# Where the weight sums of a seven-product down projection are formed: at the transfer's landing, or after each split

## The chip, the core and the metric

The kernel runs on one core of a Trainium2 chip. Time is device microseconds of one execution. The engines named are those of the profile: PE (matmul) with its weight load PEld, DVE, ACT, POOL, and SP, which here only issues transfers. Each works through its own instructions in order.

## What is computed

One layer of a hybrid decoder block on 256 tokens of width 2048, all in float32: a gated feed-forward network (SwiGLU, 5632 wide), a layer norm, a mixer (recurrence and attention), a layer norm, a second SwiGLU network, a third norm, and a gated projection.

```python
def swiglu(x, w_gate, w_up, w_down):
    return (jax.nn.silu(x @ w_gate) * (x @ w_up)) @ w_down
...
        x = layer_norm(DEEPNORM_ALPHA * x + 0.5 * swiglu(x, ffn1_w_gate[i], ffn1_w_up[i], ffn1_w_down[i]),
...
        x = layer_norm(DEEPNORM_ALPHA * x + mix, ln2_g[i], ln2_b[i])
        x = layer_norm(DEEPNORM_ALPHA * x + 0.5 * swiglu(x, ffn2_w_gate[i], ffn2_w_up[i], ffn2_w_down[i]),
                       ln3_g[i], ln3_b[i])
        x = x + jax.nn.sigmoid(x @ w_ple_gate[i]) * (p[i] @ w_ple_proj[i])
```

The change touches the product with `w_down` of both networks alone.

## The kernel before

**Precision.** Every weight tile of 256 rows x 512 columns arrives in float32 as `raw` [128, 2, 512] (512 KB). ACT casts it to a rounded `hi` (L98), DVE subtracts (L104) to get the rest, `lo`. PE multiplies with parts: three matmuls where the weight is the moving operand (activation hi x `hi`, hi x `lo`, activation lo x `hi`), two where it is the stationary one.

**The plan.** `make_plan` lists all 804 weight tiles ("entries") in the order of their use. Three pointers run through it. `load` issues the transfers of an entry, 4 entries ahead of the cast (L80). `prepare_hi` and `prepare_lo` cast and split up to AHEAD = 7 entries ahead of PE, as far as SLOTS = 7 `hi` and `lo` tiles allow. `take` hands an entry to PE. `raw` tiles come from a pool of RAWS = 9, activations and their forms from a pool `work` of 12 wide tiles. The schedule is manual: each engine runs its instructions in the order in which this code emits them, and a tile of a pool is reused when its last readers are through.

**A feed-forward network.** The 5632 columns are worked in 11 chunks (c) of 512. A chunk has 8 gate entries and 8 up entries, each group of 8 filling four PSUM banks (`group_a`). There are eight banks. When a group ends, `evac_a` empties each bank: ACT copies half (L351), DVE adds the other half (L352). After each odd chunk the down projection of the pair of chunks is done in the seven-product form (2 x 2 blocks of tokens and of weights B11, B12, B21, B22), for two column halves n, which makes 14 products per pair; each has two entries (j), 12 moving matmuls each. `make_forms` makes the token forms with ACT (L63) and DVE (L64); `product` multiplies, and adds the bank to `acc` with DVE (L408, L410). The products are interleaved with the next two chunks: one after every two gate or up entries, and in the eleventh chunk one after every entry. The eleventh chunk's own product with `w_down` is done plainly at the end (`down_last`).

**The weight side of a product.** In the order of use: p1 takes B11, p5 B11 + B12, p3 B22, p6 the sum of p5 and p3, p7 B12 + B22, p2 B21, p4 the sum p5 + p3 + p2. For p5 and p7 the entry's load is a plain transfer by SP (L75), followed by a transfer by POOL that adds the second block to the tile as it arrives (L77, `accum_op`); that one starts when the first has landed. For p6 and p4 DVE adds p3's or p2's tile onto p5's tile right before the cast (L89).

**Boundaries.** After each network and after the mixer, `ln_norm` normalises (POOL makes `rs`, L474; DVE scales, L477) and the first three entries of the next part are split by POOL into tiles of `work`.

Of the kernel before, what the change touches and what calls it, by code (L numbers as in the profile page):

```python
# [5 lines left out]
F32 = mybir.dt.float32  # L6
# [3 lines left out]
ALU = mybir.AluOpType  # L10
AX = mybir.AxisListType

P = 128
# [17 lines left out]
MAGIC = 12582912.0  # L31
AHEAD = 7
SLOTS = 7
RAWS = 9
ORDER = ("p1", "p5", "p3", "p6", "p7", "p2", "p4")
LINE = 16
PI_IN = 3.1415925
# [2 lines left out]
class Block:  # L40
# [26 lines left out]
    def load(self, q):  # L67
        e = self.plan[q]
        if e.get("load"):
            e["load"]()  # L70
        if e.get("sum"):
            return
        e["raw"] = self.tile(self.wraw, [P, 2, 512], F32, "raw")
        for k in e["parts"]:
            self.nc.sync.dma_start(e["raw"][:, k, :], e["src"][:, k, :])  # L75
        if e.get("plus") is not None:
            self.nc.gpsimd.dma_start(e["raw"], e["plus"], accum_op=ALU.add)  # L77

    def prepare_hi(self, q):
        while self.loaded < min(len(self.plan), q + 4):  # L80
            self.load(self.loaded)
            self.loaded += 1
        e = self.plan[q]
        if e.get("split"):
            e["split"]()
        if e.get("sum"):
            a, b = e["sum"]
            e["raw"] = a["raw"]
            self.nc.vector.tensor_tensor(a["raw"], a["raw"], b["raw"], op=ALU.add)  # L89
        if e["work"]:  # L90
            e["hi"], e["lo"] = self.wide_r((P, 2, 512)), self.wide_r((P, 2, 512))
        else:
            o = LINE if e["stationary"] else 0
            e["hi"] = self.tile(self.whi, [P, 1024 + 4 * LINE], F32R, "hi")[:, o:o + 1024].rearrange("p (k c) -> p k c", k=2)
            e["lo"] = self.tile(self.wlo, [P, 2, 512], F32R, "lo")
            self.live += 1
        for k in e["parts"]:
            self.nc.scalar.copy(e["hi"][:, k, :], e["raw"][:, k, :])  # L98

    def prepare_lo(self, q):  # L100
        e = self.plan[q]
        eng = self.nc.gpsimd if e["pool"] else self.nc.vector
        for k in e["parts"]:
            eng.tensor_tensor(e["lo"][:, k, :], e["raw"][:, k, :], e["hi"][:, k, :].bitcast(F32), op=ALU.subtract)  # L104

    def advance(self, need=0):
        end = min(self.limit, self.taken + AHEAD)
# [46 lines left out]
    def make_plan(self):  # L154
# [3 lines left out]
        def add(w, r0, c0, n=1, **kw):  # L158
            for j in range(n):
                plan.append({"src": self.rows2(w, r0 + 256 * j, c0), "work": False, "pool": False,  # L160
                             "parts": [slice(0, 2)], "stationary": False, **kw})
# [21 lines left out]
        def blocks(w, r0, n):  # L183
            got = {}

            def entries(kind):
                for j in range(2):
                    r, c = r0 + 256 * j, n * 512
                    at = {"p1": (0, 0), "p2": (512, 0), "p5": (0, 0), "p3": (512, 512), "p7": (0, 512)}.get(kind, (0, 0))
                    add(w, r + at[0], c + at[1], kind=kind)  # L190
                    e = got[kind, j] = plan[-1]
                    if kind in ("p5", "p7"):
                        e["plus"] = self.rows2(w, r + (512 if kind == "p7" else 0), c + 512)
                    if kind in ("p6", "p4"):
                        e["sum"] = got["p5", j], got["p3" if kind == "p6" else "p2", j]

            return [lambda kind=kind: entries(kind) for kind in ORDER]

# [26 lines left out]
        q = len(plan)  # L225
# [188 lines left out]
    def make_forms(self, h0, h1):  # L414
        nc = self.nc
        a, b = slice(0, P), slice(P, 256)
        z = self.wide((P, 2, 4, P)), self.wide((P, 2, 4, P))
        s1, s2, s3, s4 = z[0][:, 0], z[0][:, 1], z[1][:, 0], z[1][:, 1]
        self.forms = {}

        def put(kind, src):
            f = self.forms[kind] = self.wide_r((P, 2, 4, P))
            self.split(f[:, 0], f[:, 1], src)

        self.products = [(kind, n) for n in (0, 2) for kind in ORDER]
        put("p1", h0[:, :, a])
        yield
        nc.vector.tensor_tensor(s1, h1[:, :, b], h0[:, :, b], op=ALU.subtract)
        put("p5", s1)
        yield  # L430
        nc.vector.scalar_tensor_tensor(s2, s1, -1.0, h0[:, :, a], op0=ALU.mult, op1=ALU.subtract)
        nc.vector.scalar_tensor_tensor(s4, s2, -1.0, h1[:, :, a], op0=ALU.mult, op1=ALU.subtract)
        put("p3", s4)
        yield
        put("p6", s2)
        yield
        nc.vector.tensor_tensor(s3, h0[:, :, a], h0[:, :, b], op=ALU.subtract)  # L437
        put("p7", s3)
        yield
        put("p2", h1[:, :, a])  # L440
        yield
        put("p4", h1[:, :, b])
# [406 lines left out]
    def build(self):  # L849
        tc = self.tc  # L850
        with (
            tc.tile_pool(name="wraw", bufs=RAWS) as self.wraw,
            tc.tile_pool(name="whi", bufs=SLOTS) as self.whi,
            tc.tile_pool(name="wlo", bufs=SLOTS) as self.wlo,
            tc.tile_pool(name="work", bufs=12) as self.work,
            tc.tile_pool(name="const", bufs=1) as self.const,
            tc.tile_pool(name="small", bufs=2) as self.small,
            tc.tile_pool(name="work1", bufs=6) as self.work1,
# [58 lines left out]
```

## Time and profile before

| | us |
|---|---|
| median of 3 runs | 2037.47 (2035.24 to 2038.23) |
| the profiled execution | 2040.81 |
| its span, first to last instruction | 2039.0 |
| PE busy | 1916.1 |
| DVE busy | 1523.5 |
| ACT busy | 1074.1 |
| POOL busy | 243.0 |

Times in the rows further down are counted from the start of the span. A line name such as L98 is a line of the kernel before. In a table of waits, "A <- B" reads: engine and line A stood idle until B was done; behind it total us, times, longest us. In a timeline the brackets hold the idle time before an instruction and what ended it. PEclk is the granted clock of PE as a share of 2.4 GHz, so 0.50 is its other level, 1.2 GHz. Some matmul records may be missing from the trace, so counts of matmuls in a window can differ by a few.

### The profile page before, as it was taken

How to read it: one execution, taken by the hardware profiler on the slowest of the kernel's cores; microseconds unless marked ns; L12 is line 12 of the kernel's file. 1: busy time of each engine (PE TensorE's matmuls, PEld its weight loads, DVE VectorE, ACT ScalarE, POOL GpSimd, SP SyncE). 2: the span in 40 equal slices, each digit the busy share in tenths (PEclk: the TensorE clock that was granted, in tenths of full speed). 3: DMA queues.
4: the chain of work that ended last, by engine and by line, in shares of the span. 5: the costliest groups of instructions: out<-in, count | busy, mean ns of one | idle time of the engine just before them, and what ended most of it. 6: DMA issues, size and time to landing. Idle time of an engine off the chain costs nothing.

```text
span 2039.0 us, 26876 instructions
## 1 busy us (share of the span) xinstructions
PE 1916.1 (94%) x10004; PEld 1630.9 (80%) x10004; DVE 1523.5 (75%) x1889; ACT 1074.1 (53%) x1440; POOL 243.0 (12%) x173
## 2 busy tenths in 40 slices
PE   8989999989898989999999999999998999978999
PEld 7878878878787777887888898787887887867787
DVE  6676877868776798667677867787778687777874
ACT  6554544545545465456655545554545454545562
POOL 0000000000000006101010430000000000000150
PEclk9999999999999999999999999999999999989999
DMA  9757676777678775765455666877686877678663
GB/s 358 228 168 246 221 245 194 247 219 252 197 233 249 202 251 175 227 186 155 142 179 187 206 197 168 255 219 225 218 266 185 244 230 243 194 220 235 223 200 108
DMA packets 227651, 438.21 MB, mean 215 GB/s; under 512 B 13873, under 2 KB 16577, under 8 KB 227521
## 3 DMA queue, kind: packets, MB, share of 16 engines
q1 hardware_dynamic: 204736, 391.40, 57.2%
q0 software_dynamic: 22784, 45.10, 12.3%
q8 instruction: 78, 1.28, 0.3%
q14 instruction: 53, 0.43, 0.1%
HBM read 434.35 MB, written 2.10 MB: 214 GB/s over the span
## 4 chain that ended last, share of the span: by engine, by line
PE 50%; DMA 19%; DVE 17%; issue 7%; ACT 5%; POOL 1%; SPq 0%; ACTq 0%; DVEq 0%; POOLq 0%
PE mm L245 50%; DMA raw<-in_ffn_w_down_dram 19%; DVE lo L104 9%; ACT hi L98 2%; DVE w L352 2%; DVE raw L89 2%; DVE acc L410 1%; ACT w L523 1%; DVE w L524 1%; ACT w L63 1%; DVE w L538 1%; DVE w L64 1%; DMA raw<-in_ffn_w_gate_dram 0%; POOL raw L77 0%; PE mm L487 0%
## 5 line engine op out<-in xcount | busy, mean ns | idle before, releaser
L98 ACT CAST hi<-raw 128x1024 fp32r<-128x1024 f32 (+1 forms) x786 | 794.3, 1047 | 729.8 <-DMA raw<-in_ffn_w_down_dram 259.1
L245 PE MATMUL mm<-xT,hi 128*128 128x512 f32 (+1 forms) x3216 | 1120.4, 394 | 47.9 <-DVE w L352 41.7
L104 DVE TENSOR_TENSOR lo<-raw,hi 128x1024 fp32r<-128x1024 f32 (+1 forms) x786 | 957.3, 1249 | 216.9 <-ACT hi L98 211.2
L245 PE MATMUL mm<-xT,lo 128*128 128x256 f32 (+1 forms) x3216 | 894.6, 278 | 0.3 <-DVE lo L104 0.3
L245 PEld LDWEIGHTS mm<-xT,hi 128*128 128x128 f32 x3216 | 610.8, 190 | 181.4 <-DVE w L352 47.0
L245 PEld LDWEIGHTS mm<-xT,lo 128*128 128x128 f32 x3216 | 612.4, 190 | 7.8 <-DVE lo L104 2.1
L245 PE MATMUL mm<-hi,w 128*128 128x512 f32 x1464 | 495.0, 402 | 57.1 <-ACT w L63 26.7
L245 PEld LDWEIGHTS mm<-hi,w 128*128 128x128 f32 x1464 | 280.8, 192 | 131.1 <-ACT w L63 29.1
L245 PE MATMUL mm<-lo,w 128*128 128x512 f32 x732 | 292.3, 399 | 0.0
L77 POOL DMA_DIRECT2D raw<-in_ffn_w_down_dram x80 | 95.7, 1200 | 1221.0 <-DMA raw<-in_ffn_w_down_dram 438.0
L245 PE MATMUL mm<-hi,xT 128*128 128x512 f32 (+1 forms) x544 | 168.7, 386 | 0.0
L245 PEld LDWEIGHTS mm<-lo,w 128*128 128x128 f32 x732 | 141.4, 193 | 24.6
L352 DVE TENSOR_TENSOR w<-mm,w 128x256 f32<-128x256 f32 x200 | 83.6, 419 | 89.5 <-ACT w L351 89.0
L245 PEld LDWEIGHTS mm<-hi,xT 128*128 128x128 f32 x544 | 101.3, 189 | 19.2
L245 PE MATMUL mm<-lo,xT 128*128 128x512 f32 (+1 forms) x272 | 104.0, 382 | 3.6 <-DVE lo L104 3.6
L410 DVE TENSOR_TENSOR acc<-acc,mm 128x512 f32<-128x512 f32 x124 | 84.4, 680 | 19.6 <-PE mm L245 19.5
L89 DVE TENSOR_TENSOR raw<-raw,raw 128x1024 f32<-128x1024 f32 x80 | 97.3, 1217 | 0.0
L64 DVE TENSOR_TENSOR w<-w,w 128x512 fp32r<-128x512 f32 (+1 forms) x78 | 51.7, 663 | 60.0 <-ACT w L63 59.8
L351 ACT COPY w<-mm 128x256 f32<-128x256 f32 x200 | 71.7, 365 | 20.9 <-PE mm L245 17.1
L63 ACT CAST w<-w 128x512 fp32r<-128x512 f32 (+1 forms) x78 | 46.4, 595 | 63.9 <-DVE w L437 25.9
L524 DVE TENSOR_TENSOR w<-w,w 128x256 f32<-128x256 f32 x88 | 38.0, 432 | 44.2 <-ACT w L523 44.2
L523 ACT ACTIVATE w<-w 128x256 f32<-128x256 f32 x88 | 36.8, 418 | 56.1 <-DVE w L352 56.1
(136 smaller groups left out, 836.9 us busy)
## 6 DMA issues: line engine op xcount, KB each, us to landing
raw<-in_ffn_w_down_dram SPq DMA_DIRECT2D x216, 512.0 KB, 5.9
raw<-in_ffn_w_up_dram SPq DMA_DIRECT2D x176, 512.0 KB, 5.5
raw<-in_ffn_w_gate_dram SPq DMA_DIRECT2D x175, 512.0 KB, 5.9
raw<-in_w_in_dram SPq DMA_DIRECT2D x88, 512.0 KB, 4.3
raw<-in_ffn_w_down_dram POOLq DMA_DIRECT2D x80, 512.0 KB, 9.5
raw<-in_w_out_dram SPq DMA_DIRECT2D x32, 512.0 KB, 4.6
raw<-in_w_ple_gate_dram SPq DMA_DIRECT2D x32, 512.0 KB, 5.9
w<-in_ln_g_dram SPq DMA_DIRECT2D x12, 256.0 KB, 6.7
```

The costliest lines, as they stand in the source:

```text
L63: self.nc.scalar.copy(hi, src)
L64: (self.nc.gpsimd if pool else self.nc.vector).tensor_tensor(lo, src, hi.bitcast(F32), op=ALU.subtract)
L77: self.nc.gpsimd.dma_start(e["raw"], e["plus"], accum_op=ALU.add)
L89: self.nc.vector.tensor_tensor(a["raw"], a["raw"], b["raw"], op=ALU.add)
L98: self.nc.scalar.copy(e["hi"][:, k, :], e["raw"][:, k, :])
L104: eng.tensor_tensor(e["lo"][:, k, :], e["raw"][:, k, :], e["hi"][:, k, :].bitcast(F32), op=ALU.subtract)
L245: self.nc.tensor.matmul(out, lhsT=lhsT, rhs=rhs, start=start, stop=stop, skip_group_check=True)
L351: self.nc.scalar.copy(c, bank[:, 256:])
L352: self.nc.vector.tensor_tensor(dst, bank[:, :256], c, op=ALU.add)
L410: self.nc.vector.tensor_tensor(a, a, bank, op=op)
L523: nc.scalar.activation(s, g, AF.Sigmoid)
L524: nc.vector.tensor_tensor(g, g, s, op=ALU.mult)
```

## The change

The sums of the weight blocks are formed in two long-lived tiles per pair of entries. p1's entry loads both B11 (`raw`) and B12 (`other`) by SP. Right behind p1's split DVE adds `other` onto `raw` (p5's sum), and POOL's transfer then adds B22 onto `other` (p7's sum). Behind p3's split DVE adds p3's tile onto `raw` (p6's sum). Behind p6's split POOL's transfer adds B21 onto `raw` (p4's sum). p5, p6, p7 and p4 load nothing of their own. DVE still makes 80 additions and POOL still issues 80 accumulating transfers; SP's loads of `w_down` go from 216 to 176. There is one more raw tile (10), loads run 5 entries ahead instead of 4, `work` has 11 tiles instead of 12, and the sums of tokens in `make_forms` lie in tiles of the small pool `qk` (3 tiles).

```diff
-RAWS = 9
+RAWS = 10
+LOOK = 5
...
     def load(self, q):
...
-        if e.get("sum"):
+        if e.get("of"):
             return
         e["raw"] = self.tile(self.wraw, [P, 2, 512], F32, "raw")
         for k in e["parts"]:
             self.nc.sync.dma_start(e["raw"][:, k, :], e["src"][:, k, :])
-        if e.get("plus") is not None:
-            self.nc.gpsimd.dma_start(e["raw"], e["plus"], accum_op=ALU.add)
+        if e.get("beside") is not None:
+            e["other"] = self.tile(self.wraw, [P, 2, 512], F32, "raw")
+            self.nc.sync.dma_start(e["other"], e["beside"])
+
+    def raw_sum(self, a, b):
+        self.nc.vector.tensor_tensor(a, a, b, op=ALU.add)
+
+    def raw_grow(self, a, src):
+        self.nc.gpsimd.dma_start(a, src, accum_op=ALU.add)
 
     def prepare_hi(self, q):
-        while self.loaded < min(len(self.plan), q + 4):
+        while self.loaded < min(len(self.plan), q + LOOK):
...
-        if e.get("sum"):
-            a, b = e["sum"]
-            e["raw"] = a["raw"]
-            self.nc.vector.tensor_tensor(a["raw"], a["raw"], b["raw"], op=ALU.add)
+        if e.get("of"):
+            e["raw"] = e["of"][0][e["of"][1]]
...
     def prepare_lo(self, q):
...
+        for f in e.get("after", ()):
+            f()
...
             def entries(kind):
                 for j in range(2):
-                    r, c = r0 + 256 * j, n * 512
-                    at = {"p1": (0, 0), "p2": (512, 0), "p5": (0, 0), "p3": (512, 512), "p7": (0, 512)}.get(kind, (0, 0))
-                    add(w, r + at[0], c + at[1], kind=kind)
-                    e = got[kind, j] = plan[-1]
-                    if kind in ("p5", "p7"):
-                        e["plus"] = self.rows2(w, r + (512 if kind == "p7" else 0), c + 512)
-                    if kind in ("p6", "p4"):
-                        e["sum"] = got["p5", j], got["p3" if kind == "p6" else "p2", j]
+                    entry(kind, j)
+
+            def entry(kind, j):
+                r, c = r0 + 256 * j, n * 512
+                b22, b21 = self.rows2(w, r + 512, c + 512), self.rows2(w, r + 512, c)
+                at = {"p2": (512, 0), "p3": (512, 512)}.get(kind, (0, 0))
+                add(w, r + at[0], c + at[1], kind=kind)
+                e = got[kind, j] = plan[-1]
+                p1 = got["p1", j]
+                if kind == "p1":
+                    e["beside"] = self.rows2(w, r, c + 512)
+                    e["after"] = [lambda: self.raw_sum(p1["raw"], p1["other"]), lambda: self.raw_grow(p1["other"], b22)]
+                elif kind == "p3":
+                    e["after"] = [lambda: self.raw_sum(p1["raw"], e["raw"])]
+                elif kind == "p6":
+                    e["after"] = [lambda: self.raw_grow(p1["raw"], b21)]
+                if kind in ("p5", "p6", "p4", "p7"):
+                    e["of"] = p1, "other" if kind == "p7" else "raw"
...
-        z = self.wide((P, 2, 4, P)), self.wide((P, 2, 4, P))
-        s1, s2, s3, s4 = z[0][:, 0], z[0][:, 1], z[1][:, 0], z[1][:, 1]
+        s1, s2, s4 = (self.tile(self.qk, [P, 4, P], F32, "qk") for _ in range(3))
...
+        s3 = self.tile(self.qk, [P, 4, P], F32, "qk")
         nc.vector.tensor_tensor(s3, h0[:, :, a], h0[:, :, b], op=ALU.subtract)
...
-            tc.tile_pool(name="work", bufs=12) as self.work,
+            tc.tile_pool(name="work", bufs=11) as self.work,
```

The instructions move on DVE and on SP. DVE before, in the first pair of FFN 1, from gate entries ahead of p6 to p6's second entry (`raw_162` and `raw_165` are p5's tiles, `raw_185` and `raw_189` p3's, `raw_194` and `raw_197` gate's):

```order
L104 TENSOR_TENSOR lo_204_1165<-raw_194_1113,hi_203_1164 128x1024
L89 TENSOR_TENSOR raw_162_947<-raw_162_947,raw_185_1062 128x1024
L104 TENSOR_TENSOR lo_209_1189<-raw_197_1119,hi_208_1188 128x1024
L89 TENSOR_TENSOR raw_165_970<-raw_165_970,raw_189_1088 128x1024
L104 TENSOR_TENSOR lo_212_1196<-raw_162_947,hi_211_1195 128x1024
```

Each addition stands one split ahead of the split of its own sum. DVE after, at the same product (`raw_140` and `raw_149` are p1's long-lived tiles, `raw_176` and `raw_187` p3's, `qk` and `w4` forms of the tokens):

```order
L110 TENSOR_TENSOR lo_200_1125<-raw_176_1035,hi_199_1124 128x1024
L82 TENSOR_TENSOR raw_140_791<-raw_140_791,raw_176_1035 128x1024
L65 TENSOR_TENSOR w4_203_1149<-qk_180_1042,w4_203_1149 128x512
L110 TENSOR_TENSOR lo_202_1145<-raw_187_1067,hi_201_1144 128x1024
L82 TENSOR_TENSOR raw_149_820<-raw_149_820,raw_187_1067 128x1024
...
L110 TENSOR_TENSOR lo_214_1201<-raw_140_791,hi_213_1200 128x1024
```

The two additions now stand behind p3's splits, four entries ahead of p6's own. DVE after, at p1 of the same block (`raw_141` and `raw_150` hold B12, `raw_153` is a gate entry's):

```order
L110 TENSOR_TENSOR lo_163_932<-raw_140_791,hi_162_931 128x1024
L82 TENSOR_TENSOR raw_140_791<-raw_140_791,raw_141_793 128x1024
L110 TENSOR_TENSOR lo_165_952<-raw_149_820,hi_164_951 128x1024
L82 TENSOR_TENSOR raw_149_820<-raw_149_820,raw_150_822 128x1024
L110 TENSOR_TENSOR lo_168_976<-raw_153_847,hi_167_975 128x1024
```

These two additions are new on DVE; they make p5's sums. SP before, at the second column half of the same pair (`raw_266`, `raw_269` are p1's tiles, `raw_279`, `raw_282` p5's, each of which gets a transfer by POOL as well):

```order
L75 DMA raw_266_1461<-in_ffn1_w_down_dram 128x2x512
L75 DMA raw_269_1484<-in_ffn1_w_down_dram 128x2x512
L75 DMA raw_273_1504<-in_ffn1_w_gate_dram 128x2x512
L75 DMA raw_276_1510<-in_ffn1_w_gate_dram 128x2x512
L75 DMA raw_279_1532<-in_ffn1_w_down_dram 128x2x512
L75 DMA raw_282_1555<-in_ffn1_w_down_dram 128x2x512
L75 DMA raw_285_1575<-in_ffn1_w_gate_dram 128x2x512
```

And SP after, at the same place (`raw_264`, `raw_268` are p1's tiles, `raw_265`, `raw_269` those beside them):

```order
L76 DMA raw_264_1440<-in_ffn1_w_down_dram 128x2x512
L79 DMA raw_265_1442<-in_ffn1_w_down_dram 128x2x512
L76 DMA raw_268_1464<-in_ffn1_w_down_dram 128x2x512
L79 DMA raw_269_1466<-in_ffn1_w_down_dram 128x2x512
L76 DMA raw_272_1488<-in_ffn1_w_gate_dram 128x2x512
L76 DMA raw_276_1508<-in_ffn1_w_gate_dram 128x2x512
L76 DMA raw_283_1556<-in_ffn1_w_gate_dram 128x2x512
L76 DMA raw_286_1577<-in_ffn1_w_gate_dram 128x2x512
L76 DMA raw_289_1583<-in_ffn1_w_down_dram 128x2x512
```

Four loads of `w_down` stand together at p1, and none for p5: the next one, `raw_289`, is p3's.

## Rows read from the trace of the kernel before

**Rows 1.** Page, part 1: busy us, share of the span, instructions.

```profile
PE 1916.1 (94%) x10004; PEld 1630.9 (80%) x10004; DVE 1523.5 (75%) x1889; ACT 1074.1 (53%) x1440; POOL 243.0 (12%) x173
```

**Rows 2.** Page, part 4: the chain that ended last, by engine.

```profile
PE 50%; DMA 19%; DVE 17%; issue 7%; ACT 5%; POOL 1%; SPq 0%; ACTq 0%; DVEq 0%; POOLq 0%
```

**Rows 3.** Waits of ACT, whole span: total us, times, longest us.

```profile
ACT hi L98 <- DMA raw<-in_ffn_w_down_dram: 259.1, 60, 10.5
...
ACT hi L98 <- DVE raw L89: 191.5, 78, 5.5
```

**Rows 4.** Waits of PE, whole span.

```profile
PE mm L245 <- DVE w L352: 42.0, 18, 3.5
PE mm L245 <- ACT w L63: 31.1, 13, 9.3
PE mm L245 <- DVE acc L410: 25.0, 14, 3.5
```

**Rows 5.** Timeline, 124 to 136, one stall: start, us, instruction, [idle before <- releaser].

```profile
124.77 1.19 POOL L77 DMA_DIRECT2D raw<-in_ffn_w_down_dram  x1 [5.29 <-DVE w L64]
...
133.93 1.04 ACT L98 CAST hi<-raw 128x1024 fp32r<-128x1024 f32 x1 [5.40 <-DMA raw<-in_ffn_w_down_dram]
...
135.28 0.42 DVE L352 TENSOR_TENSOR w<-mm,w 128x256 f32<-128x256 f32 x1 [4.91 <-ACT w L351]
...
135.75 0.50 PE L245 MATMUL mm<-xT,hi 128*128 128x512 f32 x1 [1.86 <-DVE w L352]
```

**Rows 6.** Transfers of L77 (POOL's count, issue ns; landing), then L75's landing.

```profile
L77 POOL DMA_DIRECT2D raw<-in_ffn_w_down_dram x80: 1180/1196/1412, 85.6 to 1866.0; - x80
...
DMA to landing us min/median/max: 5.9/9.5/13.4
...
DMA to landing us min/median/max: 3.0/5.6/13.0
```

**Rows 7.** Timeline of PE: starts of products.

```profile
112.53 0.40 PE L245 MATMUL mm<-hi,w 128*128 128x512 f32 x1
120.73 0.40 PE L245 MATMUL mm<-hi,w 128*128 128x512 f32 x1
...
380.71 0.50 PE L245 MATMUL mm<-hi,w 128*128 128x512 f32 x1 [0.87 <-ACT w L63]
...
672.31 0.39 PE L245 MATMUL mm<-hi,w 128*128 128x512 f32 x1
677.79 0.42 PE L245 MATMUL mm<-hi,w 128*128 128x512 f32 x1
```

**Rows 8.** Windows: us, busy us (instructions) by engine, PEclk, DMA share, GB/s.

```profile
104.33:653.90 549.57, 515.54 (x2706) 439.64 (x2704) 415.42 (x487) 280.06 (x356) 38.20 (x32) 0.98 0.74 226
1256.14:1801.24 545.10, 514.02 (x2706) 438.20 (x2704) 415.46 (x487) 278.16 (x355) 38.25 (x32) 0.98 0.74 227
653.90:756.66 102.76, 86.23 (x411) 71.08 (x409) 85.00 (x98) 55.12 (x69) 7.16 (x6) 0.92 0.78 228
1801.24:1906.29 105.05, 87.48 (x411) 71.61 (x409) 85.11 (x98) 55.23 (x69) 7.15 (x6) 0.90 0.76 221
178.80:240.40 61.60, 61.60 (x337) 53.31 (x336) 49.62 (x58) 30.93 (x40) 4.77 (x4) 1.00 0.78 246
175.40:178.80 3.40, 3.40 (x11) 2.90 (x11) 3.30 (x8) 3.31 (x5) 0.00 (x0) 0.50 0.00 0
```

**Rows 9.** Timeline of the last chunk of FFN 1: ACT and PE.

```profile
657.99 1.04 ACT L98 CAST hi<-raw 128x1024 fp32r<-128x1024 f32 x1 [2.97 <-DMA raw<-in_ffn_w_down_dram]
...
662.20 0.79 PE L245 MATMUL mm<-hi,w 128*128 128x512 f32 x1 [8.13 <-ACT w L63]
```

**Rows 10.** Page, part 5: DVE's additions, busy us and mean ns.

```profile
L89 DVE TENSOR_TENSOR raw<-raw,raw 128x1024 f32<-128x1024 f32 x80 | 97.3, 1217 | 0.0
```

**Rows 11.** Timeline of the third boundary: POOL and PE.

```profile
1921.70 2.39 POOL L104 TENSOR_TENSOR w<-raw,w 128x1024 fp32r<-128x1024 f32 x1 [2.42 <-issue]
...
1925.34 0.63 PE L487 MATMUL mm<-ident,acc 128*128 128x128 f32 x4 [0.83 <-DVE acc L477]
```

## The prediction

> **What bounds the kernel now.** I read the busy shares first: PE is busy 94% of the span, DVE 75%, ACT 53% [rows 1]. So PE is the engine to keep fed, and the question is who makes it stop. The chain of waits answers: after PE (50%) its largest part is DMA, 19% [rows 2], although plain weight loads are issued far ahead. The table of ACT's waits names the transfers: ACT's cast (`hi`) stood 259.1 us, 60 times, behind transfers of `w_down` [rows 3]; PE's own table names only near neighbours, L352, L63 and L410, together 98.1 us [rows 4]. One stall in the timeline joins them [rows 5]: POOL issues an accumulating transfer at 124.77; ACT, which works in order, stops 5.40 us at the cast that needs it and goes on at 133.93; the copy L351 that empties a PSUM bank stood behind that cast, so DVE's L352 waited 4.91 for it; PE waited 1.86 for the bank. Why always these transfers: an accumulating one starts only when the plain load of the same tile has landed, and then takes 5.9 / 9.5 / 13.4 us (min / median / max) itself, behind loads that take 3.0 / 5.6 / 13.0 [rows 6]; the cast wants it two products later at most.
>
> **What the stalls cost.** A product and two gate/up entries on clean ground take 120.73 − 112.53 = 8.20 us; in the last chunk a product and one entry take 677.79 − 672.31 = 5.48 [rows 7]. So an entry is 2.72 and a product 2.76. A pair of chunks, from its first product to the next pair's, is 32 entries and 14 products: 125.7. The fourth pair of an FFN ends an entry earlier (123.0). The last chunk, from its first product on, is 15 entries and 14 products: 79.4. Against that [rows 8]: the four pairs of FFN 1 took 549.57 where 3 × 125.7 + 123.0 = 500.1, 49.5 too long; those of FFN 2 545.10, 45.0 too long; the last chunks 102.76 and 105.05, 23.4 and 25.7 too long. In all 143.6 us. It holds the 98.1 of waits and some 45 of lost clock: after a stop the granted clock is 0.50 for a while, as in 175.40 to 178.80, where 11 matmuls took the whole 3.40 us [rows 8].
>
> **The change, part by part.**
>
> *p5 and p7.* Their second half no longer comes by a transfer that ACT meets on arrival. B11 and B12 are both plain loads, made with p1; DVE adds them for p5; POOL grows the second tile to p7's sum, four products (16 entries in the order of the plan) before it is cast. In time: 16 entries at a quarter of a slot, 8.20 / 4 = 2.05 us, are 33 us, against a landing of 13.4 at worst [rows 6]. This takes ACT off the transfers in pairs, at all three places where it stood. The chunk entries between are now ahead of what they need, and I take the pairs down to their clean length but for 2 us each: a short wait of 0.87 as at 380.71, which follows ACT's form casts and no transfer [rows 7], and part of a stretch at half clock behind it. Estimate: 8 × 2 = 16 stay, 94.5 − 16 = **78.5 gained**. Bounds: 94.5 if nothing stays; about half if the waits for banks are DVE's own (first rival).
>
> *p6 and p4.* p6's addition on DVE moves forward to p3's `lo`, so ACT's 191.5 us behind additions [rows 3] lose their cause; these waits are mostly slack that ACT has, since PE's table shows little behind them, so I count nothing. p4's sum becomes an accumulating transfer, issued behind p6's `lo`, 11 entries or 23 us ahead of its cast in the pairs. In the last chunk the lead is 9 entries of 5.48 / 3 = 1.83, 16.4 us, against 13.4 plus two issues of 1.2 [rows 6]: just enough.
>
> *The last chunk.* Its worst stop is PE's 8.13 at 662.20, behind a cast that waited for a transfer at 657.99 [rows 9]; such stops go too. But DVE is busy 85.00 of these 102.76 us, and 85.11 of 105.05 [rows 8], and its work stays: as many additions, 80 of 1217 ns [rows 10], splits and evacuations as before. So DVE is what is late next, and the floor is 85, not 79.4. I take 88 (97% busy; bounds 85 and 95, the second at DVE 89%): 14.8 + 17.0 = **31.8 gained**.
>
> *Does DVE hold the pace in the pairs?* From 178.80 to 240.40 no transfer is waited for: PE was busy 61.60 of 61.60 us with DVE at 49.62 (81%), through a change of group [rows 8]. So 81% on DVE need not stop PE.
>
> *Loads.* 40 plain loads of 512 KB fall away (p5 and p7 shared a start with p1's tile); the accumulating transfers stay 80. The DMA share in the clean stretch is 0.78, and nobody waited for plain loads there: worth nothing on the path. The tenth raw tile and the look-ahead of 5 instead of 4 entries pay for two pairs of tiles that now live through five to seven products. In the built order SP's plain loads stay at least 8 entries ahead of their cast (7 before), 16 us against 13.0 at worst [rows 6].
>
> *One work tile fewer.* At the three boundaries POOL splits three entries into work tiles. At the third boundary one already waited for its tile and ran 2.39 us at 1921.70, ahead of the small `rs` on POOL; PE lost 0.83 to it at 1925.34 [rows 11]. With 11 tiles the built order puts one such split late at boundaries 1 and 2 (0.83 each) and a second one at the third (2.4 more): 4.1. In the mixer one DVE operation gains a wait on POOL, for which no row stands: I take 1, between 0 and the 2.39 of that split, since it is a product of two tiles of the same size. Together **5.1 lost**, between 0 (the tiles come free in time) and 8 (a full split of 2.39 at each boundary and the mixer's 1).
>
> **Sum.** 78.5 + 31.8 − 5.1 = 105.2. The profiled execution took 2040.8 (span 2039.0 and 1.8 around it), which becomes 1935.6; it is 3.4 above the median of the runs, so I forecast 2037.5 − 105.2 = 1932.3.
>
> **A rule against it.** PE stops for banks that DVE and ACT empty late [rows 4]. The Trainium skill, "Perfetto Trace Analysis", section Optimization Strategy, says that consistent bubbles, the same gap repeating on the engine that should be saturated, can mean that SBUF or PSUM has no room for the next tile. By that rule the cure would be banks, not transfers. The mechanism here would be: eight banks, four of a group and up to three of products, so that the next group's first bank waits for L352 or L410 whatever ACT meets. The clean stretch speaks against it, since a group changes in it with no stop.
>
> **Rivals.**
> 1. *DVE's order.* The added sums stand directly behind a `lo` on DVE, 1.2 us each, two in a row per product, and L352 and L410 stand behind them; or p4's transfer, with its narrow lead, is late in the last chunk. For: DVE has 18% to spare in the pairs and next to none in the last chunk. Against: the clean stretch has p6's additions in it. If half of the waits for L352 and L410 stays, half of (42.0 + 25.0) / 98.1 of the 110.3 gained is lost, 38: **1970** (1955 to 2000).
> 2. *Banks* (the mechanism beside the rule). All of those waits stay, 68% of the gain: 75 lost, **2008**.
> 3. *Nothing moves.* As many accumulating transfers go through POOL as before; if they queue behind DVE and now hold ACT at p4 and p7 instead of p5 and p7, the stalls change place only: **2037**. Against: 23 and 33 us of lead.
> 4. *Slower: raw tiles.* Four of the ten tiles are held from p1 to p4 and two of them to p7, so loads of gate and up rotate through six. If a load is issued later than 13.0 / 2.05 = 6.3 entries before its cast, the stall of today meets every entry. Price: 20 blocks (two column halves of ten pairs), two extra stops each, of some 4 us (a wait of 1.86 [rows 5] and about as much again at half clock): 160, less the 110: **2087**. Against: the lead of 8 in the built order, which holds only if the tiles come free on time.
>
> **How the numbers follow.** My forecast has 0.64 (1910 to 1950: 85 in the last chunks and nothing left in the pairs on one side, 95 in the last chunks and 8 of boundary cost on the other), a better time than 1910 has 0.02, DVE's order 0.17, banks 0.06, nothing moves 0.04, raw tiles 0.07. The range runs from 1908 to 1990: it holds the forecast and most of the first rival and leaves out some 0.2. Faster by over 0.2% (about what a measurement of this kernel can tell from no change): 0.64 + 0.02 + 0.17 + 0.06 = 0.89; the same 0.04; slower 0.07.
>
> **What would show it.** In the profile after: ACT's waits for `w_down` transfers near 0 instead of 259.1, with still 80 accumulating transfers; a pair of 127 to 128 us and a last chunk near 88 with DVE over 95% busy; PE's waits for L352 and L410 (other line numbers then) down to a few us; the granted clock near 1.00 in the FFNs; at the boundaries a POOL split ahead of `rs` and a stop of PE of 1 to 3 us. If ACT's waits for transfers vanish and those for banks stay, the banks or DVE's order were the cause, and pairs stay over 130. If ACT waits for gate and up loads, the raw tiles are too few. If ACT still waits for `w_down`, the leads are wrong.

## The result and the profile after

The changed kernel takes 1921.0 us (median of 4 runs, 1920.29 to 1922.0), the kernel before, beside it, 2037.85: a ratio of 0.9425 (95% interval 0.9407 to 0.9442), 5.8% less time. The forecast was 1932. The profiled execution took 1922.0 us with a span of 1919.9, against 2039.0 before.

The page of the profile after, its parts 1 and 4 (the chain of waits by engine):

```profile
PE 1878.9 (98%) x10004; PEld 1614.0 (84%) x10004; DVE 1522.9 (79%) x1889; ACT 1090.7 (57%) x1440; POOL 242.4 (13%) x173
...
PE 87%; DVE 7%; issue 2%; ACT 2%; DMA 1%; POOL 1%; SPq 0%; ACTq 0%; DVEq 0%; POOLq 0%
```

DVE, ACT and POOL are about as busy in microseconds as before [rows 1]; what went is PE's time: it stands idle for 41.0 us of the span instead of 122.9, 81.9 less, and its busy time is 37.2 less for the same matmuls, since fewer of them run at half clock (PEclk below). DMA has left the chain: 1% instead of 19% [rows 2], PE itself has 87% of it. ACT's waits and then PE's, whole span (total us, times, longest us):

```profile
ACT hi L104 <- DVE raw L82: 16.4, 10, 2.1
...
ACT hi L104 <- DMA raw<-in_ffn_w_down_dram: 7.9, 6, 1.8
```

```profile
PE mm L263 <- DVE acc L428: 11.0, 4, 3.5
PE mm L263 <- DVE xT L65: 5.2, 1, 5.2
PE mm L505 <- DVE acc L495: 4.8, 3, 3.1
PE mm L263 <- ACT w L64: 4.3, 6, 0.7
```

ACT's 259.1 us behind growing tiles are 7.9, its 191.5 behind additions 16.4 [rows 3]. PE's waits for L352 (now L370) are gone from the table, those for L63 (now L64) are 4.3 instead of 31.1, those for L410 (now L428) 11.0 instead of 25.0 [rows 4]. POOL still issues 80 accumulating transfers; they land in 5.7 / 7.4 / 11.0 us instead of 5.9 / 9.5 / 13.4 [rows 6]:

```profile
L85 POOL DMA_DIRECT2D raw<-in_ffn_w_down_dram x80: 1180/1196/1665, 97.0 to 1755.4; - x80
...
DMA to landing us min/median/max: 5.7/7.4/11.0
```

Windows of the same four stretches as [rows 8], from first product to first product (us, busy us and instructions by engine, PEclk, DMA share, GB/s): the four pairs of each network, then the two last chunks.

```profile
104.89:606.54 501.65, 500.27 (x2706) 432.50 (x2705) 422.48 (x500) 292.01 (x364) 38.31 (x32) 1.00 0.80 235
1197.00:1697.00 500.00, 500.00 (x2706) 432.25 (x2705) 420.52 (x497) 290.87 (x363) 38.28 (x32) 1.00 0.80 234
606.54:695.39 88.85, 82.90 (x410) 69.58 (x409) 77.17 (x87) 51.27 (x61) 7.22 (x6) 0.96 0.82 243
1697.00:1784.78 87.78, 81.82 (x411) 68.80 (x409) 77.19 (x87) 51.28 (x61) 7.22 (x6) 0.98 0.83 247
```

In the four pairs of the second network PE is busy for 500.00 of 500.00 us, at full clock. The account of the spans, term by term:

| | before | after | gained | forecast |
|---|---|---|---|---|
| four pairs, FFN 1 | 549.57 | 501.65 | 47.9 | |
| four pairs, FFN 2 | 545.10 | 500.00 | 45.1 | |
| pairs together | | | 93.0 | 78.5 |
| last chunks | 102.76 + 105.05 | 88.85 + 87.78 | 31.2 | 31.8 |
| all the rest | 736.5 | 741.6 | -5.1 | -5.1 |
| span | 2039.0 | 1919.9 | 119.1 | 105.2 |

### The profile page after: what moved, and what is told of

It is laid out like the page before. It is cut to its first block, busy times and chain, and to the rows that moved or that the text cites. A ratio compares the mean times of both kernels' runs of the same rounds, so it can differ in the third digit from the quotient of the medians.

```text
span 1919.9 us, 26885 instructions
## 1 busy us (share of the span) xinstructions
PE 1878.9 (98%) x10004; PEld 1614.0 (84%) x10004; DVE 1522.9 (79%) x1889; ACT 1090.7 (57%) x1440; POOL 242.4 (13%) x173
## 4 chain that ended last, share of the span: by engine, by line
PE 87%; DVE 7%; issue 2%; ACT 2%; DMA 1%; POOL 1%; SPq 0%; ACTq 0%; DVEq 0%; POOLq 0%
PE mm L263 86%; DVE lo L110 3%; DVE raw L82 1%; DVE w L370 1%; ACT hi L104 1%; DMA raw<-in_w_in_dram 0%; DMA raw<-in_ffn_w_gate_dram 0%; PE mm L505 0%; DVE w L556 0%; ACT w L64 0%; POOL w L110 0%; DVE w L65 0%; DMA raw<-in_ffn_w_down_dram 0%; DVE acc L495 0%; DVE acc L428 0%
## 5 line engine op out<-in xcount | busy, mean ns | idle before, releaser
L104 ACT CAST hi<-raw 128x1024 fp32r<-128x1024 f32 (+1 forms) x786 | 809.6, 1049 | 545.3 <-PE mm L263 470.6
L263 PE MATMUL mm<-xT,hi 128*128 128x512 f32 (+1 forms) x3216 | 1104.8, 390 | 6.2 <-DVE xT L65 5.2
L263 PE MATMUL mm<-hi,w 128*128 128x512 f32 x1464 | 483.2, 394 | 13.3 <-DVE acc L428 11.0
L263 PEld LDWEIGHTS mm<-hi,w 128*128 128x128 f32 x1464 | 276.5, 189 | 76.2 <-ACT hi L104 13.7
L428 DVE TENSOR_TENSOR acc<-acc,mm 128x512 f32<-128x512 f32 x124 | 84.9, 684 | 100.8 <-PE mm L263 100.8
L370 DVE TENSOR_TENSOR w<-mm,w 128x256 f32<-128x256 f32 x200 | 83.6, 419 | 28.1 <-ACT w L369 27.6
L82 DVE TENSOR_TENSOR raw<-raw,raw 128x1024 f32<-128x1024 f32 x80 | 97.8, 1222 | 1.4
L64 ACT CAST w<-qk 128x512 fp32r<-128x512 f32 (+1 forms) x42 | 25.5, 609 | 83.6 <-DVE qk L455 40.4
L542 DVE TENSOR_TENSOR w<-w,w 128x256 f32<-128x256 f32 x88 | 38.0, 432 | 43.4 <-ACT w L541 43.4
L508 ACT ACTIVATE qk<-mm,par 128x128 f32<-128x128 f32 x96 | 36.1, 456 | 54.3 <-PE mm L505 54.1
```

Of the source, the lines that this page charges most:

```text
L64: self.nc.scalar.copy(hi, src)
L82: self.nc.vector.tensor_tensor(a, a, b, op=ALU.add)
L263: self.nc.tensor.matmul(out, lhsT=lhsT, rhs=rhs, start=start, stop=stop, skip_group_check=True)
L370: self.nc.vector.tensor_tensor(dst, bank[:, :256], c, op=ALU.add)
L428: self.nc.vector.tensor_tensor(a, a, bank, op=op)
L508: nc.scalar.activation(z[:, q, :], bank[:, q * P:(q + 1) * P], AF.Identity, bias=self.par[:, p0 + 16 + kb:p0 + 17 + kb], scale=self.par[:, ...
```

## The experiments

Twelve kernels ran, four at a time on one chip. The kernel before took 2043.64 us beside the first four, 2037.79 beside the second and 2038.34 beside the third, so ratios to it are compared across groups.

### Is it the growing tile? The second transfers left out

```diff
-        if e.get("plus") is not None:
-            self.nc.gpsimd.dma_start(e["raw"], e["plus"], accum_op=ALU.add)
```

> The kernel before, with the accumulating second transfers of p5 and p7 left out (B12's share in p5's sum and B22's in p7's are missing; all else stands, the additions of p6 and p4 right ahead of their casts too). Theory (ACT stood at casts whose tile was still growing): pairs fall from 137 to 126 us, the last chunks from 103 to about 88, and no boundary cost is added: 1915 us, or a little less than the changed kernel's 1921. Rival, the places of DVE's additions: what ACT waits behind them (191.5 us) stays and holds pairs above 130: 1950 to 1970. Rival, banks: PE's waits for L352 and L410 stay near 67 us: about 1990.

Measured: 1911.28 us, ratio 0.9357 (0.9342 to 0.9371). Its windows, one pair and one last chunk:

```profile
606.82:692.27 85.45, 80.76 (x410) 67.53 (x409) 79.51 (x89) 50.11 (x61) 0.00 (x0) 1.00 0.66 219
...
231.51:357.52 126.01, 125.97 (x682) 108.68 (x681) 105.67 (x126) 72.37 (x91) 0.00 (x0) 1.00 0.64 217
```

and its waits, ACT's behind the additions and PE's longest:

```profile
ACT hi L96 <- DVE raw L87: 173.5, 72, 4.0
```

```profile
PE mm L243 <- DVE acc L408: 8.3, 6, 2.6
```

The stalls are gone, with the additions of p6 and p4 where they were and with the same eight banks. So those additions and the banks were not what stopped PE. Both rivals fall. What this run cannot tell is whether the transfers' traffic or their landing counted, since it takes both away.

### Lead or traffic? p7's transfer issued later

```diff
                 if kind == "p1":
...
-                    e["after"] = [lambda: self.raw_sum(p1["raw"], p1["other"]), lambda: self.raw_grow(p1["other"], b22)]
+                    e["after"] = [lambda: self.raw_sum(p1["raw"], p1["other"])]
...
                 elif kind == "p6":
-                    e["after"] = [lambda: self.raw_grow(p1["raw"], b21)]
+                    e["after"] = [lambda: self.raw_grow(p1["other"], b22), lambda: self.raw_grow(p1["raw"], b21)]
```

> The changed kernel with one thing moved: POOL's transfer that grows p7's tile is issued behind p6's split, 4 entries (8.2 us) ahead of its cast instead of 16; the traffic is the same. Theory (the lead of the transfer against its landing of 5.9 to 13.4 us decides): ACT's waits for w_down transfers come back, at p7 alone, 20 blocks of some 2 to 3 us of PE each: 1960 us (1940 to 1985). Rival, 21 MB less traffic or the deeper loads made the gain: 1921, pairs stay at 125.7.

Measured: 2008.8 us, ratio 0.9832 (0.9815 to 0.9848). ACT's wait, and the windows of a pair and of a last chunk:

```profile
ACT hi L104 <- DMA raw<-in_ffn_w_down_dram: 169.9, 25, 12.1
```

```profile
238.88:370.59 131.71, 127.79 (x683) 110.08 (x681) 105.98 (x126) 72.60 (x91) 9.67 (x8) 0.99 0.77 224
630.37:735.03 104.66, 86.17 (x410) 71.74 (x409) 77.43 (x87) 50.63 (x61) 8.48 (x7) 0.92 0.73 209
```

The same instructions and bytes, one transfer of two issued 12 entries later, and some seven tenths of the gain are lost: lead, not traffic. The direction was as expected, the loss was twice as large and outside the range given. A last chunk loses all that it had gained (104.66 against 102.76 in the kernel before): the lead of 4 entries in the pairs is there one of 3 entries, 3 x 1.83 = 5.5 us, less than the quickest landing, 5.9 in the kernel before [rows 6] and 5.8 in this one.

The same transfer issued behind p3's split, in the middle:

```diff
                 if kind == "p1":
...
-                    e["after"] = [lambda: self.raw_sum(p1["raw"], p1["other"]), lambda: self.raw_grow(p1["other"], b22)]
+                    e["after"] = [lambda: self.raw_sum(p1["raw"], p1["other"])]
                 elif kind == "p3":
-                    e["after"] = [lambda: self.raw_sum(p1["raw"], e["raw"])]
+                    e["after"] = [lambda: self.raw_sum(p1["raw"], e["raw"]), lambda: self.raw_grow(p1["other"], b22)]
```

> The changed kernel with p7's growing transfer issued behind p3's split: 8 entries ahead of its cast (16 us in the pairs, 6 entries or 11 us in the last chunk) instead of 16; with 4 entries the time was 2009 us. Theory (lead against a landing of 7 us at the median and 11 to 14 at worst): pairs stay at 125.7, the last chunks rise to 90 to 95: 1925 us (1920 to 1937). Rival, order on POOL and SP rather than the lead: pairs already rise above 128, 1945 or more.

Measured: 1922.82 us, ratio 0.9431 (0.9416 to 0.9445); the changed kernel beside it on that chip 1922.78 (0.9433, 0.9414 to 0.9452). Last chunks:

```profile
607.28:696.01 88.73, 82.77 (x411) 69.50 (x409) 77.18 (x87) 51.28 (x61) 7.22 (x6) 0.96 0.81 243
1697.60:1785.48 87.88, 81.95 (x411) 68.83 (x409) 77.18 (x87) 51.29 (x61) 7.22 (x6) 0.98 0.82 248
```

8 entries of lead are as good as 16, and in the last chunk 6 (11 us) as good as 12, where I had expected a few us of waiting. So between 4 and 8 entries lies the point from which the lead is enough. The run of the changed kernel that it was measured against:

> The changed kernel once more, as the measure for the three runs beside it on the same chip: 1921 us; pairs 125.7, last chunks 88 to 89.

It took 1922.78 us (1919.76 to 1927.55). The profiled execution was the slowest of them, 1927.55. Its pairs in FFN 1 took 501.65 us as before, but its last chunks more than the 88 to 89 expected:

```profile
606.07:695.63 89.56, 83.61 (x411) 70.02 (x409) 77.45 (x87) 51.40 (x61) 7.22 (x6) 0.96 0.81 241
1697.04:1787.51 90.47, 84.53 (x410) 70.79 (x409) 77.53 (x87) 51.29 (x61) 7.22 (x6) 0.94 0.81 237
```

So last chunks of one and the same kernel lie between 87.78 and 90.47 us.

### The sizes alone, and the sums alone

All of the change's sizes on the kernel before: 10 raw tiles, loads 5 entries ahead, 11 work tiles, token sums in `qk` (the two diffs below, together):

> The kernel before with the change's sizes alone: 10 raw tiles, loads 5 entries ahead instead of 4, 11 work tiles, the token sums in the small pool; the transfers and sums as before. Theory: the accumulating transfers start one entry (2.05 us) earlier, which takes 2 of the 4 us or so of each of ACT's 60 waits, so a third of the loss goes, and the boundaries cost 5: about 2000 us (1980 to 2025). Rival, that depth of loading is what the change gained by: 1921 to 1935. Rival, sizes do nothing: 2038 to 2043.

Measured: 1968.36 us, ratio 0.9637 (0.9621 to 0.9652). That is a gain of some 74 us, and more than I gave it. Two further runs split it, the first without the token sums:

```diff
-RAWS = 9
+RAWS = 10
+LOOK = 5
...
-        while self.loaded < min(len(self.plan), q + 4):
+        while self.loaded < min(len(self.plan), q + LOOK):
...
-            tc.tile_pool(name="work", bufs=12) as self.work,
+            tc.tile_pool(name="work", bufs=11) as self.work,
```

> The kernel before with 10 raw tiles, loads 5 entries ahead and 11 work tiles; transfers, sums and the token sums' tiles as before. It splits the run with all of the change's sizes (1968 us), from which it differs by the token sums alone. If one entry more of lead for the growing tiles did it: 1965 to 1975. If the token sums' own small tiles did it: 2030 to 2040.

Measured: 1966.98 us, ratio 0.9638 (0.9599 to 0.9677). And the token sums alone:

```diff
-        z = self.wide((P, 2, 4, P)), self.wide((P, 2, 4, P))
-        s1, s2, s3, s4 = z[0][:, 0], z[0][:, 1], z[1][:, 0], z[1][:, 1]
+        s1, s2, s4 = (self.tile(self.qk, [P, 4, P], F32, "qk") for _ in range(3))
...
+        s3 = self.tile(self.qk, [P, 4, P], F32, "qk")
```

> The kernel before with the token sums in the small pool and nothing else changed (9 raw, 12 work tiles). Theory (lead): within 5 us of the kernel before, 2037. If the forms were held up by work tiles: 1975 to 2010.

Measured: 2038.12 us, ratio 1.0001 (0.9981 to 1.002). So it is the tenth raw tile and the loads issued one entry earlier, together; no run takes these two apart. Waits of ACT, then of PE, with the deeper loads alone:

```profile
ACT hi L99 <- DVE raw L90: 193.6, 77, 5.5
ACT hi L99 <- DMA raw<-in_ffn_w_down_dram: 160.3, 48, 7.0
```

```profile
PE mm L246 <- DVE acc L411: 20.0, 11, 3.0
PE mm L246 <- DVE w L353: 13.8, 7, 5.2
PE mm L246 <- ACT w L64: 9.6, 7, 5.3
```

ACT's waits for growing tiles fall from 259.1 us to 160.3, the longest from 10.5 to 7.0 [rows 3]; PE's for these three lines from 98.1 us in 45 stops to 43.4 in 25 [rows 4]. PE has splits in store, so it sees only the end of each of ACT's waits, 98.1 / 45 = 2.2 us on average before; one entry of 2.05 us more in lead can take much of that. This reading fits the numbers, but no run varied the store itself.

The other half, the sums as changed with the old sizes:

```diff
-RAWS = 10
-LOOK = 5
+RAWS = 9
+LOOK = 4
...
-            tc.tile_pool(name="work", bufs=11) as self.work,
+            tc.tile_pool(name="work", bufs=12) as self.work,
```

> The changed kernel with the old sizes: 9 raw tiles, loads 4 entries ahead, 12 work tiles; the sums as changed, the token sums in the small pool. In the built order most plain loads stand 7 to 9 entries ahead, one per block of products 5 (10 us). Theory (the lead of the accumulating transfers is what counts): pairs stay within 2 us of 125.7 and the boundaries give their 5 us back: 1921 us (1912 to 1935). Rival, the tenth tile made the gain: 1965 to 1990. Rival, the long-lived tiles leave too few of nine for the plain loads: ACT waits for gate and up loads, pairs above 137, over 2037.

Measured: 1917.98 us, ratio 0.9401 (0.9369 to 0.9433). The pairs of both networks:

```profile
103.66:605.33 501.67, 500.25 (x2706) 432.23 (x2705) 422.52 (x500) 292.01 (x364) 38.30 (x32) 1.00 0.81 234
1192.65:1692.65 500.00, 500.00 (x2706) 432.55 (x2705) 420.49 (x497) 290.80 (x363) 38.28 (x32) 1.00 0.80 234
```

They are the pairs of the changed kernel within 0.02 us. Nine raw tiles are enough for the plain loads, though each block's sums hold four of them for long. The same kernel beside the changed one:

> The changed sums with the old sizes (9 raw tiles, loads 4 ahead, 12 work tiles) beside the changed kernel on one chip. Theory: the only difference is the boundaries, 1.0 + 1.1 + 2.3 us in the profiles so far: 4.4 us faster, 1916.5. Rival: the shorter lead of the plain loads costs it back: the same.

Measured: 1919.16 us, ratio 0.9413 (0.94 to 0.9425), 3.6 us under the changed kernel's 1922.78; the intervals overlap, and two of the changed kernel's four runs, at 1919.8, were nearly as fast, so the runs don't settle the difference. The profiles show where one lies: PE's stops at the boundaries, below, 0.8 us in this kernel's profile against 4.8. So the sums alone bring the whole gain, the deeper loads alone some 70 us of it, and once the sums are there the deeper loads bring nothing.

| ratio to the kernel before | old sizes | new sizes |
|---|---|---|
| old sums | 1 | 0.9637 |
| new sums | 0.9401, 0.9413 | 0.9425, 0.9433 |

### What is left in the last chunk

p4's sum by DVE instead of a transfer, behind p2's split:

```diff
-                elif kind == "p6":
-                    e["after"] = [lambda: self.raw_grow(p1["raw"], b21)]
+                elif kind == "p2":
+                    e["after"] = [lambda: self.raw_sum(p1["raw"], e["raw"])]
```

> The changed kernel with p4's sum made by DVE again (behind p2's split) instead of a transfer: 40 accumulating transfers fewer, 120 additions on DVE instead of 80. Theory (DVE sets the pace of the last chunk, the pairs have room): pairs stay at 125.7, DVE's share there goes to 85%; the last chunks grow by 4 additions of 1.22 us each, 4.9: 1931 us. Rival, the remaining transfers of p4 arrive late in the last chunk: it falls from 88 to about 80, 1905 us. Rival, neither: 1921.

Measured: 1926.66 us, ratio 0.9428 (0.9407 to 0.9448), not to be told from the changed kernel's 0.9425. The last chunk of FFN 1, and a pair:

```profile
606.75:697.10 90.35, 83.78 (x411) 69.96 (x409) 81.52 (x91) 51.24 (x61) 2.39 (x2) 0.96 0.68 211
...
232.43:358.11 125.68, 125.68 (x682) 108.73 (x681) 110.15 (x130) 73.05 (x91) 4.77 (x4) 1.00 0.72 218
```

DVE has 4.4 us more to do in the last chunk. At 90.35 us it is 1.5 longer than in the changed kernel's first profile, but within the 87.78 to 90.47 of that kernel's two profiles: no cost shows. So p4's transfers did not hold it up, and it isn't DVE's total either, which is 81.52 of 90.35. In the pairs even 110.15 of 125.68 (88%) costs nothing.

Every second gate and up entry of the last chunk split by POOL:

```diff
-                        add(w, 256 * j, c * 512, stationary=True)
+                        add(w, 256 * j, c * 512, stationary=True, pool=step == 1 and j % 2 == 1)
```

> The changed kernel with every second gate and up entry of the last chunk split by POOL (2.4 us each, 16 in all) instead of DVE (1.22 us). Theory (DVE's order sets what is left in the last chunk, which takes 88 us against a clean 79.4): it gives 10 us of DVE's work away per last chunk and falls to 80 to 84: 1921 - 12 = 1909 us (1903 to 1915). Rival, POOL's slow splits come late or hold the growing transfers behind them in POOL's order: the last chunk rises to 90 or more, 1925 to 1940.

Measured: 1933.49 us, ratio 0.9477 (0.9445 to 0.9509): slower, the rival's side, with 92.95 us in the last chunk of FFN 1. The costliest groups of lines in the last chunk of FFN 1: first those of DVE in the changed kernel (mean ns after the busy us), then those of DVE and POOL in this one:

```profile
L110 DVE TENSOR_TENSOR lo<-raw,hi 128x1024 fp32r<-128x1024 f32 x43 | 50.8, 1220 | 0.0
...
L82 DVE TENSOR_TENSOR raw<-raw,raw 128x1024 f32<-128x1024 f32 x6 | 7.3, 1222 | 0.1
```

```profile
L110 DVE TENSOR_TENSOR lo<-raw,hi 128x1024 fp32r<-128x1024 f32 x36 | 52.6, 1495 | 0.0
...
L82 DVE TENSOR_TENSOR raw<-raw,raw 128x1024 f32<-128x1024 f32 x6 | 9.5, 1589 | 0.1
...
L110 POOL TENSOR_TENSOR lo<-raw,hi 128x1024 fp32r<-128x1024 f32 x7 | 19.5, 2786 | 29.2 <-ACT hi L104 29.2
```

DVE makes 36 splits there instead of 43 and is busy longer with them, since they take 1495 ns on average instead of 1220. Nothing was given away. The timeline shows how: DVE's splits ahead of a POOL split, a POOL split, and DVE's beside it.

```profile
621.35 3.49 DVE L110 TENSOR_TENSOR lo<-raw,hi 128x1024 fp32r<-128x1024 f32 x3
...
638.41 2.42 POOL L110 TENSOR_TENSOR lo<-raw,hi 128x1024 fp32r<-128x1024 f32 x1 [8.12 <-ACT hi L104]
...
638.47 4.57 DVE L110 TENSOR_TENSOR lo<-raw,hi 128x1024 fp32r<-128x1024 f32 x2
```

Three splits alone take 3.49 us, two beside POOL's 4.57. Two alone take 2.35 (at 599.66 in the changed kernel), so DVE lost 2.2 us, nearly the whole of POOL's 2.42, to be spared one split of 1.22. The rival's reasons were others (late splits, transfers held on POOL); ACT waited only 3.5 us for `w_down` in this run.

The timeline of DVE in the changed kernel, just ahead of the first stop, and PE's row at it (start us, us, instruction, [idle before <- releaser]):

```profile
611.22 1.22 DVE L110 TENSOR_TENSOR lo<-raw,hi 128x1024 fp32r<-128x1024 f32 x1
612.36 1.22 DVE L82 TENSOR_TENSOR raw<-raw,raw 128x1024 f32<-128x1024 f32 x1
613.49 1.22 DVE L110 TENSOR_TENSOR lo<-raw,hi 128x1024 fp32r<-128x1024 f32 x1
614.63 1.22 DVE L82 TENSOR_TENSOR raw<-raw,raw 128x1024 f32<-128x1024 f32 x1
615.76 1.22 DVE L110 TENSOR_TENSOR lo<-raw,hi 128x1024 fp32r<-128x1024 f32 x1
...
619.60 0.68 DVE L428 TENSOR_TENSOR acc<-acc,mm 128x512 f32<-128x512 f32 x1
```

```profile
620.43 0.47 PE L263 MATMUL mm<-hi,w 128*128 128x512 f32 x1 [2.00 <-DVE acc L428]
```

Split, addition, split, addition, split stand in a row, and the `acc` that gives PE its bank back stands behind them. The second stop, 3.5 us, stands behind the same five (from 656.01). That suggests taking these additions away where the lead allows it. In the last pair of each network p6's sum is grown by POOL behind p5's split (old sizes):

```diff
+                elif kind == "p5" and r0 == (NCH - 3) * 512:
+                    e["after"] = [lambda: self.raw_grow(p1["raw"], b22)]
-                elif kind == "p3":
+                elif kind == "p3" and r0 != (NCH - 3) * 512:
                     e["after"] = [lambda: self.raw_sum(p1["raw"], e["raw"])]
```

> The changed sums with the old sizes, and in the last pair of each network (whose products run in the last chunk) p6's sum grown by a POOL transfer of B22 behind p5's split instead of DVE's addition of p3's tile: 4 additions fewer per last chunk. Theory (PE's two stops there stand behind a run of split, addition, split, addition on DVE): both stops of 2 to 4 us and the stretch at half clock behind one go, the last chunks fall from 88.5 to 82 or 83: 1905 us (1900 to 1911). Rival, the transfer, 6 entries or 11 us ahead, lands late: ACT waits for w_down again, 1918 to 1930.

Measured: 1903.1 us (1902.61 to 1903.86), ratio 0.9333 (0.9321 to 0.9346), the fastest of all, 16 us under the same kernel without it (1919.16) and 20 under the changed one. The last chunks:

```profile
606.39:688.02 81.63, 79.95 (x410) 67.66 (x409) 72.55 (x83) 51.01 (x61) 10.83 (x9) 1.00 1.00 287
1687.55:1769.21 81.66, 79.98 (x410) 67.70 (x409) 72.55 (x83) 51.08 (x61) 10.85 (x9) 1.00 1.00 287
```

and its `acc` at the place of the stop, with the row ahead of it:

```profile
616.58 0.69 DVE L65 TENSOR_TENSOR w<-qk,w 128x512 fp32r<-128x512 f32 x1 [0.69 <-ACT w L64]
617.18 0.68 DVE L430 TENSOR_TENSOR acc<-acc,mm 128x512 f32<-128x512 f32 x1
```

Counted from the `acc` before it (610.47 here, 610.62 in the changed kernel) it comes after 6.71 us instead of 8.98: 2.27 earlier, the two additions at 1.13 from start to start. PE's waits for this line fall from 11.0 us in 4 stops to 2.4 in 2, the clock stays up (PEclk 1.00 instead of 0.96 and 0.98), and the last chunk is within 2.3 us of the clean 79.4, though the DMA share is 1.00 in it. The rival was right that ACT waits for `w_down` again, 8.8 us in 8 stops where it was 0.2 in one without the edit, but PE did not stop for it. The same kernel without the edit has last chunks of 88.77 and 89.53, so 4.6 us less of DVE's work brought 7 to 8, where 4.4 more in another place had no cost that shows. DVE's total therefore does not set the length; that the place of the additions does fits both runs and the timeline, but no run moved them and kept their number.

### The boundaries

POOL and PE at the third boundary of the changed kernel:

```profile
1800.19 4.69 POOL L110 TENSOR_TENSOR w<-raw,w 128x1024 fp32r<-128x1024 f32 x2 [4.79 <-DMA raw<-in_w_ple_gate_dram]
1804.84 0.56 POOL L492 TENSOR_TENSOR rs<-ve,mhalf 128x1 f32<-128x1 f32 x1
...
1806.13 0.63 PE L505 MATMUL mm<-ident,acc 128*128 128x128 f32 x4 [3.13 <-DVE acc L495]
```

Two splits now run directly ahead of `rs` where one did, and PE waits 3.13 us instead of 0.83 [rows 11]. Over all three boundaries it is 4.8 us in 3 stops (PE's table above), 4.0 more than before. The fastest kernel, with 12 work tiles, is back at 0.8 in one stop.

## Why the prediction came out right

*What bounded the kernel.* Right: ACT's casts behind tiles that were still growing. Leaving the transfers out cleared PE (126.01 a pair), cutting one transfer's lead brought the waits back (169.9 us on ACT), 8 entries of lead were enough again. The parts of the loss were right in kind too: 81.9 us of idle time and 37.2 of busy time went, where the forecast saw 98.1 of waits and some 45 of lost clock.

*Pairs.* The one term that was mis-sized: 93.0 us gained instead of 78.5. The step that failed is the residue, 8 x 2 us. I took the short wait of 0.87 at 380.71 [rows 7] for the form casts' own, with no transfer behind it, as its releaser is L63. ACT's rows in the kernel before, just ahead of it, show the same stall:

```profile
379.09 1.05 ACT L98 CAST hi<-raw 128x1024 fp32r<-128x1024 f32 x1 [4.28 <-DMA raw<-in_ffn_w_down_dram]
380.04 0.61 ACT L63 CAST w<-w 128x512 fp32r<-128x512 f32 x1
```

The form cast was late because ACT had stood 4.28 us at the cast ahead of it, behind a transfer. After the change all pairs but the first are clean, and the whole residue is 1.6 us in the first network and nothing in the second (501.65 and 500.00, where clean pairs make 500.1). This term is why the time came out 11 us under the forecast (13.6 between the profiled executions).

*Last chunk.* The number was right (88, measured 88.85 and 87.78), its reason only half; that it came out so close was in part luck. DVE was to be busy 97% there; it was busy 77.17 us, 87%. The 85.00 of before [rows 8] was no floor: DVE ran 98 instructions in that window and 87 in the same window after. Eight of the eleven are the evacuation of the group ahead of the window, which DVE was late with before. Its first row before, inside the window that starts at 653.90, and after, ahead of 606.54:

```profile
659.34 0.42 DVE L352 TENSOR_TENSOR w<-mm,w 128x256 f32<-128x256 f32 x1 [3.06 <-ACT w L351]
```

```profile
602.59 0.42 DVE L370 TENSOR_TENSOR w<-mm,w 128x256 f32<-128x256 f32 x1 [0.57 <-ACT w L369]
```

The other three are a split and two additions; the change makes two of p5's sums ahead of its window. What is left is the order on DVE, as the first rival had it, but in the last chunk alone: the run with p6's sums grown by POOL brought 7 to 8 us a chunk by taking two additions each out from ahead of two of the `acc` lines.

*p4's narrow lead* (16.4 us against 13.4 and the issues) was enough: ACT waited 7.9 us for `w_down` in the whole span, and making p4's sum on DVE made nothing faster.

*DVE in the pairs.* Right, it need not stop PE: it was busy 420 to 422 of 500 us (84%) there, and 88% of a pair in the run with p4's sums on DVE, where PE was busy for all of it.

*Boundaries.* 5.1 forecast, 5.1 measured outside the networks' products, the last digit by luck: 4.0 is PE's at the three boundaries (4.1 forecast). Of the other 1.1, which I had put into the mixer, half is at the start, where the first product comes at 104.89 instead of 104.33. But that start varies by more between two profiles of one and the same kernel (103.66 and 105.83, the new sums with the old sizes), so the runs put the 1.1 down to nothing.

*The sizes.* I gave them a servant's part: a tenth tile and deeper loads that pay for the tiles held longer. Neither half of that was so. The sums run as well with nine tiles, and without the new sums the tenth tile and the earlier loads take away more than half of the loss. I had the lead as the cause, but didn't ask what the old kernel would do with one entry more of it.

*Rivals.* Nothing moves, and raw tiles: both fell, the second even with nine tiles. Banks fell with the first experiment. The rule of the Trainium skill beside it ("Perfetto Trace Analysis", section Optimization Strategy: consistent bubbles can mean too little SBUF or PSUM for the next tile) names what can be, and here it was not PSUM: eight banks are enough as soon as ACT comes in time. For SBUF the trace agrees in part: one more raw tile of 512 KB, with loads one entry earlier, was worth some 70 us to the old kernel. The earlier issue of the growing transfers cured the whole, with the old sizes too.

## What to carry to other kernels

When a waiting engine's releasers are near neighbours of many kinds, follow one stall back until something appears that an in-order engine could not go past; here three lines held PE up; two are shown above behind a transfer that could start only when its tile had just been loaded, and without those transfers PE's waits for the third fell from 25.0 us to 8.3. Compare the time between issue and use with the longest landing in the trace, in the fastest stretch of the kernel, and lengthen it until it exceeds that; here a lead of 8 entries instead of 16 cost nothing. Before crediting an edit's main idea, run its buffer sizes alone: part of the gain may be there for one line. And on an engine that still has a share of time free, an addition placed just ahead of what frees a bank can cost more than its own length (here 7 to 8 us for four of 1.22).

## What the runs showed of the hardware

POOL and DVE slow each other: in the last chunk with POOL's splits DVE's take 1495 ns on average instead of 1220 and its additions 1589 instead of 1222, and POOL's 2786 where one at a boundary took 2390 [rows 11]. The mean hides that few are hit hard: two DVE splits beside one of POOL took 4.57 us, three away from it 3.49. The Trainium skill, "SBUF — State Buffer", section Who interferes with whom, says that a DVE instruction with two SBUF inputs contends with a GpSimd instruction that reads SBUF; these rows agree, and give the price.

At a DMA share of 1.00 (287 GB/s, the last chunks of the fastest kernel) PE waited 1.7 us in the first of these chunks, none of it behind a transfer; ACT waited there for `w_down` 5.0 us in 4 stops. The growing transfers stand 6 entries or more (11 us) ahead of their casts there. And the 80 accumulating transfers of the changed kernel landed in 7.4 us at the median, those of the kernel before in 9.5. With p7's transfer late, so that two are issued in a row, it was 8.1 with the same bytes; how much of the 9.5 was the 40 more plain loads is open.
